# Top-k search of a sparse attention: which query tiles ScalarE searches, and where the mask is finished

## The chip, the cores and the metric

The program runs on one core of a Trainium2 chip. The metric is the device time of one execution in microseconds (us). Three runs of the kernel before were timed: the median is 2041.14 us (2039.17 to 2042.02).

## The reference

One decoder layer over 1024 tokens of width 1024: a mixer with four branches and a gated convolutional FFN, each behind an RMS norm. The branch that matters here (D) is a sparse attention. Eight small indexer heads give every query a score for every earlier key; the 256 best keys of each query are kept, ties broken towards the lower index; then four heads attend to the kept keys alone:

```python
score = jnp.einsum('bqhk,bqh->bqk', jax.nn.relu(logits), wi[:, t0:t1])
score = jnp.where(jnp.arange(kl)[None, None, :] <= qpos[None, :, None], score, -jnp.inf)
_, idx = lax.top_k(score, topk)          # topk = 256
k_sel = gather(k, idx)
...
p = jax.nn.softmax(jnp.where(valid, s, -jnp.inf), axis=-1)
```

The other inputs of the four branches are slices of one projection `z = h @ w_in`.

## The kernel before

The 1024 queries are eight tiles of 128 (t = 0 to 7), and tile t sees 128(t+1) keys. Tiles 0 and 1 keep every key, so a search is needed for tiles 2 to 7, with 384 to 1024 columns each. The scores of these six tiles lie side by side in the SBUF tile `score`; `sct(t)` is tile t's part.

The 256th best score of each query (a row) is found bit by bit, without sorting. `key` holds first the upper 16 bits of the score (15 steps), then, for the rows' tied candidates, the lower 16 bits (16 steps). One step counts the row's keys that reach a trial value and keeps or drops one bit. Two engines search different tiles side by side:

- `search_v` (L611 to L621), on VectorE, takes the tiles of `V_T`, here 7, 6, 3 and 2. Per step it has one count per tile (`count`, L604 to L609, recorded as L607 with a short read of the accumulator) and three small instructions over all of its tiles (L616, L619, L620).
- `search_a` (L623 to L638), on ScalarE, takes the tiles of `A_T`, here 5 and 4. Per step and tile it has one Sign pass that sums (L634), and two 1-column instructions (L635, L636). At its end L638 hands over its thresholds as `T`.

Between the searches, L652 to L661 on VectorE count again, mark the keys equal to the threshold found so far (L656) and put the lower 16 bits of those into `key` (L659). ScalarE's second search starts from these keys and from `kq` (L627, L628). After both, L664 to L668 join the halves to one threshold `Tx`.

The loop over ties (L670 to L680) then writes the mask. Per tile: a count of what is above the threshold (L607), the keys equal to it (L674), a running sum over them (L675, a scan), the first ones up to 256 (L677), their union with those above (L679), all on VectorE, and last, on ScalarE, L680, which turns 1 and 0 into 0 and -1e30 in `score`. The attention (L684 to L730) adds that to its logits on VectorE (L710), tile 7 first.

While VectorE searches, the other engines project. `proj` (L358) takes one 128-column block of `w_in`: the block is loaded through SyncE's queue into `wraw`, ScalarE rounds it to a high part `whi` (L187), GpSimd (POOL) takes the low part `wlo` (L188), and TensorE (PE) multiplies both with the activations in two halves of 24 matmuls (L367). ScalarE empties each half out of PSUM (L526 `pl`; L536 and L537 `chi`, `czf`; L399 to L404 `sw`, `r`), and GpSimd does the rotary arithmetic (L405 to L409). `wraw`, the pair `whi`/`wlo` and the PSUM tile `mm` have two buffers each. In between TensorE runs the conditioning projections, `adaps` (L205) and `adac` (L217), with ScalarE's copy `adae` (L214) between the two.

A scheduler decides, when the program is built, in which order each engine's instructions stand; then each engine runs its own list strictly in that order, and an instruction that waits holds all that stand behind it.

Of the kernel before, what the change touches and what calls it, by code (L numbers as in the profile page):

```python
# [16 lines left out]
AF = mybir.ActivationFunctionType  # L17
OP = mybir.AluOpType
# [8 lines left out]
NT = S // P  # L27
# [4 lines left out]
NEG = -1.0e30  # L32
# [59 lines left out]
               ("inv16", 1), ("inv32", 1), ("sgn", 1), ("nb", 6), ("dn", 6), ("nn", 6)):  # L92
    PKN = _pk(_n, _w)

V_T = [7, 6, 3, 2]
A_T = [5, 4]
NV = len(V_T)


# [13 lines left out]
def tile_hybrid_block(ctx, tc, x, pos, ada, pk, cst, w_in, w_br, w_out, w_up, w_dn, out):  # L113
# [6 lines left out]
    V, G, A, PE = nc.vector, nc.gpsimd, nc.scalar, nc.tensor  # L120
# [28 lines left out]
    epsc, halfpi, onec, negc = zcol[:, 0:1], zcol[:, 1:2], zcol[:, 2:3], zcol[:, 4:5]  # L149
# [121 lines left out]
    with ExitStack() as mix:  # L271
# [11 lines left out]
        with pool("xtp", 1) as xtp, pool("adp", 8) as adp:  # L283
# [4 lines left out]
            for t in range(NT):  # L288
                xt = adp.tile([P, D], F32, name="xt", tag="w")
                dma(xt, x[t * P:(t + 1) * P, :])  # L290
                if t == 0:
# [9 lines left out]
                                op0=OP.mult, op1=OP.add)  # L301
# [15 lines left out]
            for m in range(4):  # L317
                mod_affine(m, A1, B1, "g1", pmm, "mm", stp, "st", adp)
                for j in (2 * m, 2 * m + 1):
                    V.tensor_scalar(out=xT[:, j, :], in0=xT[:, j, :], scalar1=A1[:, j:j + 1],  # L320
                                    scalar2=B1[:, j:j + 1], op0=OP.mult, op1=OP.add)
# [6 lines left out]
            for kind in ("inv16", "inv32"):  # L328
# [4 lines left out]
                                op0=OP.mult, op1=OP.add)  # L333
                V.tensor_scalar(out=kk, in0=kk, scalar1=MAGIC, scalar2=None, op0=OP.subtract)
                for c in (_C1, _C2, _C3):
                    V.scalar_tensor_tensor(out=ang, in0=kk, scalar=-float(c), in1=ang,
                                           op0=OP.mult, op1=OP.add)
                V.tensor_scalar(out=ang, in0=ang, scalar1=3.1415925, scalar2=-3.1415925,
                                op0=OP.min, op1=OP.max)
# [151 lines left out]
        with pool("scp", 1) as scp, ExitStack() as scx:  # L491
            score = scp.tile([P, NTOT], F32, name="score")
            sct = lambda t: score[:, off[t - 2]:off[t - 1]]
            with pool("iqk", 4) as iqk, pool("itm", 3) as itm:
# [5 lines left out]
                for h in range(8):  # L500
# [3 lines left out]
                    for t in range(2, NT):  # L504
# [5 lines left out]
                        if h == 0:  # L510
                            V.tensor_scalar(out=sct(t), in0=tmp[:, :n], scalar1=wiT[:, t, h:h + 1],
                                            scalar2=zcol[:, 3:4], op0=OP.mult, op1=OP.add)
# [74 lines left out]
            with pool("rad", 1) as rad, pool("radj", 1) as radj, pool("rada", 1) as rada:  # L587
                key = rad.tile([P, NTOT], BF, name="key")
                keyt = lambda t: key[:, off[t - 2]:off[t - 1]]
# [56 lines left out]
                for t in A_T + V_T:  # L646
                    c = off[t - 2]
                    V.tensor_scalar(out=keyt(t), in0=score.bitcast(BF)[:, 2 * c + 1:2 * off[t - 1]:2],
                                    scalar1=sg_[:, kc(t):kc(t) + 1], scalar2=None, op0=OP.mult)
# [17 lines left out]
                                       op0=OP.logical_shift_left, op1=OP.bitwise_or)  # L667
                V.tensor_tensor(out=Tx, in0=Ti[:, 0, :].bitcast(F32), in1=sg_, op=OP.mult)  # L668

                for t in range(2, NT):  # L670
                    n = (t + 1) * P
                    tx = Tx[:, kc(t):kc(t) + 1]
                    g_ = count(cnt, sct(t), t, tx, OP.is_gt)
                    V.tensor_scalar(out=keyt(t), in0=sct(t), scalar1=tx, scalar2=None, op0=OP.is_equal)  # L674
                    V.tensor_tensor_scan(out=sct(t), data0=ones[:, 0:1].to_broadcast([P, n]), data1=keyt(t),  # L675
                                         initial=cnt[:, kc(t):kc(t) + 1], op0=OP.mult, op1=OP.add)
                    V.scalar_tensor_tensor(out=keyt(t), in0=sct(t), scalar=float(TOPK), in1=keyt(t),  # L677
                                           op0=OP.is_le, op1=OP.mult)
                    V.tensor_tensor(out=keyt(t), in0=keyt(t), in1=g_[:, :n], op=OP.add)  # L679
                    A.activation(sct(t), keyt(t), AF.Identity, scale=-NEG, bias=negc)  # L680

            adx.close()

# [624 lines left out]
```

## Time and profile before

| | before |
|---|---|
| median of three runs | 2041.14 us |
| profiled execution: its own time | 2039.7 us |
| its span, first to last instruction | 2037.9 us |
| PE, VectorE, ScalarE, POOL busy | 89%, 63%, 45%, 37% of the span |
| mean granted TensorE clock | 0.949 |
| chain that ended last: PE, VectorE, POOL | 47%, 22%, 13% |

The steps below are told by their start in us from the first instruction of the span: the first search runs from 182 to 252, the compaction to 267, the second search to 354, the loop over ties to 388. The sparse attention's first logits come at 456. A number that a row gives in brackets at its end is the idle time of the engine just before, and what ended it.

### The profile page before, as it was taken

The numbers are of one execution on the slowest core, as the hardware profiler recorded it, in microseconds if no ns is written. First come the engines' busy times: TensorE is split into PE (matmuls) and PEld (weight loads), VectorE is DVE, ScalarE is ACT, GpSimd is POOL, SyncE is SP. The second block draws the span as 40 slices with busy tenths as digits, with TensorE's granted clock in tenths as the row PEclk, the third lists the DMA queues.
The fourth block names the chain that finished last, engine by engine and source line by source line (L and its number), as shares of the span: only waits on it lengthen the run. The fifth ranks groups of instructions, "written<-read, shape, count | busy, mean of one in ns | idle before, by whom it ended". The sixth has DMA issues, their size and how long they took to land.

```text
span 2037.9 us, 23289 instructions
## 1 busy us (share of the span) xinstructions
PE 1819.0 (89%) x8528; PEld 1406.0 (69%) x8528; DVE 1283.4 (63%) x1896; ACT 908.7 (45%) x1648; POOL 748.8 (37%) x425
## 2 busy tenths in 40 slices
PE   6888887498999999899999899589999989799998
PEld 3655665376767776677777667368777777678886
DVE  6759999505999847684013764586676766743632
ACT  5555666246555645464123454443333333343331
POOL 0102145281111110012105611587676676555440
PEclk8988989699999999899999999799999999999999
DMA  8354422444513251513123634112122212364731
GB/s 309 95 150 162 177 100 77 134 91 120 168 54 122 79 150 58 135 47 109 62 84 134 217 127 152 52 52 81 66 82 73 73 72 73 104 229 164 238 124 62
DMA packets 78307, 237.18 MB, mean 116 GB/s; under 512 B 10673, under 2 KB 14897, under 8 KB 78065
## 3 DMA queue, kind: packets, MB, share of 16 engines
q1 hardware_dynamic: 78192, 235.69, 36.1%
q8 instruction: 67, 1.10, 0.2%
q14 instruction: 48, 0.39, 0.1%
HBM read 179.82 MB, written 55.84 MB: 116 GB/s over the span
## 4 chain that ended last, share of the span: by engine, by line
PE 47%; DVE 22%; POOL 13%; DMA 9%; issue 5%; ACT 4%; SPq 0%; DVEq 0%; POOLq 0%; ACTq 0%
PE mm L367 18%; PE dps L1186 11%; DVE junkb L607 6%; POOL wblk L942 6%; DMA wr<-in_w_up 5%; PE ups L1071 4%; PE av L488 3%; PE sc L468 2%; PE yps L995 2%; DVE hc L874 2%; PE brp L927 2%; PE tr L478 2%; POOL wsum L1051 2%; POOL wr L1051 2%; POOL wlo L188 1%
## 5 line engine op out<-in xcount | busy, mean ns | idle before, releaser
L188 POOL TENSOR_TENSOR wlo<-wraw,whi 128x1024 fp32r<-128x1024 f32 x104 | 267.5, 2576 | 856.7 <-ACT whi L187 831.9
L367 PE MATMUL mm<-hH,whi 128*128 128x512 f32 x864 | 356.0, 412 | 47.0 <-ACT whi L187 29.9
L367 PE MATMUL mm<-hL,whi 128*128 128x512 f32 x864 | 353.3, 409 | 1.2 <-DVE hL L323 1.2
L367 PE MATMUL mm<-hH,wlo 128*128 128x512 f32 x864 | 351.7, 407 | 2.9 <-POOL wlo L188 2.9
L1071 PE MATMUL ups<-th,wblk 128*128 128x512 f32 x1320 | 313.3, 394 | 16.5 <-DVE th L1099 7.9
L1071 PEld LDWEIGHTS ups<-th,wblk 128*128 128x128 f32 x1320 | 250.3, 190 | 74.1 <-DVE th L1099 11.5
L367 PEld LDWEIGHTS mm<-hH,whi 128*128 128x128 f32 x864 | 167.8, 194 | 94.1 <-ACT whi L187 30.4
L367 PEld LDWEIGHTS mm<-hH,wlo 128*128 128x128 f32 x864 | 167.3, 194 | 41.4 <-POOL wlo L188 4.2
L187 ACT CAST whi<-wraw 128x1024 fp32r<-128x1024 f32 x122 | 127.5, 1048 | 149.5 <-DMA wraw<-in_w_dn 60.8
L367 PEld LDWEIGHTS mm<-hL,whi 128*128 128x128 f32 x864 | 168.3, 195 | 36.4 <-issue 2.6
L942 POOL TENSOR_TENSOR wblk<-wr,wblk 128x512 fp32r<-128x512 f32 x84 | 137.3, 1654 | 33.1 <-ACT wblk L941 33.0
L1071 PE MATMUL ups<-h2h,wblk 128*128 128x512 f32 x352 | 124.1, 416 | 26.5 <-DVE ub L1141 25.6
L1200 DVE TENSOR_TENSOR actl<-actw,acth 128x512 fp32r<-128x512 f32 x42 | 65.2, 1578 | 105.7 <-ACT acth L1199 105.7
L607 DVE TENSOR_SCALAR_CACHE_REDUCE junkb<-key,cf 128x1024 bf16<-128x1024 uint16 (+3 forms) x124 | 117.3, 946 | 4.3
L1186 PE MATMUL dps<-wlo,acth 128*128 128x512 f32 x336 | 104.0, 389 | 0.6 <-POOL wlo L188 0.6
L1186 PE MATMUL dps<-whi,acth 128*128 128x512 f32 x336 | 104.0, 389 | 0.0
L1186 PE MATMUL dps<-whi,actl 128*128 128x512 f32 x336 | 103.9, 389 | 0.0
L1071 PEld LDWEIGHTS ups<-h2h,wblk 128*128 128x128 f32 x352 | 69.5, 198 | 49.4 <-DVE ub L1141 32.3
L941 ACT CAST wblk<-wsum 128x512 fp32r<-128x512 f32 x66 | 38.8, 618 | 143.3 <-DVE wsum L1051 142.6
L1128 DVE SCALAR_TENSOR_TENSOR ub<-ub,pkt 128x1023 f32<-128x1023 f32 x44 | 79.0, 1796 | 24.7 <-ACT ub L1127 24.7
L1127 ACT ACTIVATE ub<-ub,pkt 128x1024 f32<-128x1024 f32 x44 | 54.5, 1238 | 89.2 <-DMA act_s<-ub 76.4
L942 POOL TENSOR_TENSOR wblk<-wsum,wblk 128x512 fp32r<-128x512 f32 x66 | 91.8, 1404 | 0.0
(592 smaller groups left out, 3498.5 us busy)
## 6 DMA issues: line engine op xcount, KB each, us to landing
wraw<-in_w_in SPq DMA_DIRECT2D x54, 512.0 KB, 4.0
adaw<-in_ada SPq DMA_DIRECT2D x48, 512.0 KB, 5.8
wr<-in_w_up SPq DMA_DIRECT2D x44, 512.0 KB, 3.3
wraw<-in_w_dn SPq DMA_DIRECT2D x44, 512.0 KB, 3.5
sg_s<-gt SPq DMA_DIRECT2D x44, 256.0 KB, 2.4
sgl<-sg_s SPq DMA_DIRECT2D x22, 512.0 KB, 3.4
act_s<-ub SPq DMA_DIRECT2D x22, 512.0 KB, 2.6
actw<-act_s SPq DMA_DIRECT2D x42, 256.0 KB, 4.1
```

The lines of the kernel that those rows point to most:

```text
L187: A.copy(hi, raw)
L188: (E or G).tensor_tensor(out=lo, in0=raw, in1=hi.bitcast(F32), op=OP.subtract)
L367: PE.matmul(ps, a[:, ks], b[:, k, cs], start=(n == 0), stop=(n == 3 * NK - 1))
L488: PE.matmul(av[64 * hh:64 * hh + 64, :], vals[hh](kt), aTs[hh][:, kt, :], start=(kt == 0), stop=(kt == t), tile_position=(0, 64 * hh))
L607: V.tensor_scalar(out=j[:, :n], in0=src, scalar1=scal, scalar2=None, op0=op, op1=OP.add, accum_out=dst[:, kc(t):kc(t) + 1])
L942: E.tensor_tensor(out=b[:, 1], in0=r, in1=b[:, 0].bitcast(F32), op=OP.subtract)
L1051: tt = lambda E, o, a, b, op: E.tensor_tensor(out=o, in0=a, in1=b, op=op)
L1071: PE.matmul(ps, u[:, ks], v[:, k, :], start=(n == 0), stop=(n == 11))
L1127: A.activation(u, c, AF.Identity, bias=pc("fb", m, m + 1), scale=w(2))
L1128: V.scalar_tensor_tensor(out=u[:, 1:], in0=c[:, 0:S - 1], scalar=w(1), in1=u[:, 1:], op0=OP.mult, op1=OP.add)
L1186: PE.matmul(ps[:, cs], a[:, tl], b[:, cs], start=(chunk == 0 and n == 0 and i == 0), stop=(chunk == len(CH) - 1 and n == len(ops) - 1 and ...
L1200: V.tensor_tensor(out=lo, in0=raw, in1=hi.bitcast(F32), op=OP.subtract)
```

## The change

```diff
-V_T = [7, 6, 3, 2]
-A_T = [5, 4]
+V_T = [6, 4, 3, 2]
+A_T = [7, 5]
...
-                for t in range(2, NT):
+                for t in range(NT - 1, 1, -1):
                     n = (t + 1) * P
                     tx = Tx[:, kc(t):kc(t) + 1]
                     g_ = count(cnt, sct(t), t, tx, OP.is_gt)
...
                     V.tensor_tensor(out=keyt(t), in0=keyt(t), in1=g_[:, :n], op=OP.add)
-                    A.activation(sct(t), keyt(t), AF.Identity, scale=-NEG, bias=negc)
+                    V.tensor_scalar(out=sct(t), in0=keyt(t), scalar1=-NEG, scalar2=NEG, op0=OP.mult, op1=OP.add)
```

ScalarE searches tiles 7 and 5 (1024 and 768 columns) in place of 5 and 4 (768 and 640). VectorE searches 6, 4, 3 and 2. The loop over ties goes from tile 7 down to tile 2, and its last operation is VectorE's.

The order of the instructions on POOL and on SyncE does not change in a row. Three places move.

ScalarE at the end of the second search (`T_2702` is the second search's thresholds, `whi` the next block of weights, `chi` and `czf` a projection's halves). Before:

```order
L638 ACTIVATE T_2702<-Bn 128x2
L680 ACTIVATE score<-key,zcol 128x384
L536 ACTIVATE chi<-mm 128x512
L537 ACTIVATE czf<-mm 128x512
L680 ACTIVATE score<-key,zcol 128x512
L680 ACTIVATE score<-key,zcol 128x640
L680 ACTIVATE score<-key,zcol 128x768
L680 ACTIVATE score<-key,zcol 128x896
L187 CAST whi<-wraw 128x1024 x2
L680 ACTIVATE score<-key,zcol 128x1024
L686 ACT_TABLE_LOAD
```

And now (`junka` is a Sign pass of the search):

```order
L634 ACTIVATE junka,sgs<-key,Bn 128x1024
L636 ACTIVATE Bn<-sgn,Bn 128x1
L635 ACTIVATE sgn<-sgs,kq 128x1
L634 ACTIVATE junka,sgs<-key,Bn 128x768
L636 ACTIVATE Bn<-sgn,Bn 128x1
L635 ACTIVATE sgn<-sgs,kq 128x1
L636 ACTIVATE Bn<-sgn,Bn 128x1
L638 ACTIVATE T_2702<-Bn 128x2
L686 ACT_TABLE_LOAD
L187 CAST whi<-wraw 128x1024 x2
L536 ACTIVATE chi<-mm 128x512
L537 ACTIVATE czf<-mm 128x512
```

The six L680 are gone, and the two `whi` stand right behind the thresholds and a table load; the halves `chi` and `czf` that stood behind the first L680 now stand in the search, some rows ahead of this piece.

ScalarE between the two searches (`T_2701` is the first search's thresholds; `adae` is what TensorE's `adac` waits for). Before:

```order
L638 ACTIVATE T_2701<-Bn 128x2
L526 ACT_TABLE_LOAD
L526 ACTIVATE pl<-mm 128x512
L634 ACTIVATE junka,sgs<-key,Bn 128x768
L634 ACTIVATE junka,sgs<-key,Bn 128x640
L187 CAST whi<-wraw 128x1024
L526 ACTIVATE pl<-mm 128x512
L214 COPY adae<-adaps 128x512
L222 COPY md<-adac 128x4
L635 ACTIVATE sgn<-sgs,kq 128x1 x2
```

And now:

```order
L638 ACTIVATE T_2701<-Bn 128x2
L634 ACTIVATE junka,sgs<-key,Bn 128x1024
L526 ACTIVATE pl<-mm 128x512
L634 ACTIVATE junka,sgs<-key,Bn 128x768
L187 CAST whi<-wraw 128x1024
L526 ACTIVATE pl<-mm 128x512
L635 ACTIVATE sgn<-sgs,kq 128x1 x2
L214 COPY adae<-adaps 128x512
L636 ACTIVATE Bn<-sgn,Bn 128x1 x2
L222 COPY md<-adac 128x4
L634 ACTIVATE junka,sgs<-key,Bn 128x1024
```

The second search's first Sign pass stands ahead of a projection's `pl`, and `adae` now stands behind L635, which waits for `kq`.

VectorE's loop over ties, its first rows. Before:

```order
L668 TENSOR_TENSOR Tx<-Ti,sg__2698 128x6
L607 TENSOR_SCALAR junkb,cnt<-score,Tx 128x384
L674 TENSOR_SCALAR key<-score,Tx 128x384
L674 TENSOR_SCALAR key<-score,Tx 128x512
L675 SCALAR_TENSOR_TENSOR score<-ones,cnt,key 128x384
L674 TENSOR_SCALAR key<-score,Tx 128x640
L677 SCALAR_TENSOR_TENSOR key<-score,key 128x384
L674 TENSOR_SCALAR key<-score,Tx 128x768
L679 TENSOR_TENSOR key<-key,junkb 128x384
L674 TENSOR_SCALAR key<-score,Tx 128x896
```

And now:

```order
L668 TENSOR_TENSOR Tx<-Ti,sg__2698 128x6
L607 TENSOR_SCALAR junkb,cnt<-score,Tx 128x1024
L674 TENSOR_SCALAR key<-score,Tx 128x1024
L674 TENSOR_SCALAR key<-score,Tx 128x896
L675 SCALAR_TENSOR_TENSOR score<-ones,cnt,key 128x1024
L674 TENSOR_SCALAR key<-score,Tx 128x768
L677 SCALAR_TENSOR_TENSOR key<-score,key 128x1024
L674 TENSOR_SCALAR key<-score,Tx 128x640
L679 TENSOR_TENSOR key<-key,junkb 128x1024
L674 TENSOR_SCALAR key<-score,Tx 128x512
L680 TENSOR_SCALAR score<-key 128x1024
```

The widest tile comes first, each tile ends with its L680, and behind the loop VectorE's list is the same as before.

## Rows read from the trace of the kernel before

**Rows 1.** What TensorE waited for, 166 to 460 us: total, times, longest.

```profile
PE mm L367 <- ACT whi L187: 29.9, 1, 29.9
```

**Rows 2.** TensorE's timeline, 348 to 380 us: start, duration (us).

```profile
379.53 0.80 PE L367 MATMUL mm<-hH,whi 128*128 128x512 f32 x1 [29.93 <-ACT whi L187]
```

**Rows 3.** ScalarE's timeline behind the second search.

```profile
346.62 0.20 ACT L638 ACTIVATE T<-Bn 128x2 f32<-128x2 f32 x1
358.71 0.62 ACT L680 ACTIVATE score<-key,zcol 128x384 f32<-128x384 bf16 x1 [11.89 <-DVE key L679]
359.23 0.58 ACT L536 ACTIVATE chi<-mm 128x512 fp32r<-128x512 f32 x1
...
377.50 1.04 ACT L680 ACTIVATE score<-key,zcol 128x896 f32<-128x896 bf16 x1 [4.16 <-DVE key L679]
378.45 1.98 ACT L187 CAST whi<-wraw 128x1024 fp32r<-128x1024 f32 x2
...
388.36 1.28 ACT L686 ACT_TABLE_LOAD   x1
```

**Rows 4.** The chain that ended last, 355 to 400 us: start, duration.

```profile
360.38 1.36 POOL czf L538
...
362.88 5.34 DMA wraw<-in_w_in
```

**Rows 5.** Groups by line and shape, 150 to 460 us: busy us, mean ns, idle before.

```profile
L607 DVE TENSOR_SCALAR_CACHE_REDUCE junkb<-key,cf 128x1024 bf16<-128x1024 uint16 x16 | 20.5, 1279 | 0.5
...
L634 ACT ACTIVATE junka<-key,Bn 128x768 bf16<-128x768 uint16 x16 | 14.8, 925 | 15.8 <-DVE key L659 15.8
...
L634 ACT ACTIVATE junka<-key,Bn 128x640 bf16<-128x640 uint16 x16 | 13.1, 818 | 1.2 <-DVE key L659 1.2
...
L607 DVE TENSOR_SCALAR_CACHE_REDUCE junkb<-key,T 128x640 bf16<-128x640 int16 x1 | 0.9, 879 | 0.0
```

**Rows 6.** ScalarE's timeline between the searches.

```profile
254.80 0.93 ACT L634 ACTIVATE junka<-key,Bn 128x768 bf16<-128x768 uint16 x1 [15.80 <-DVE key L659]
...
259.31 0.57 ACT L214 COPY adae<-adaps 128x512 f32<-128x512 f32 x1
...
268.60 0.48 ACT L635 ACTIVATE sgn<-sgs,kq 128x1 f32<-128x1 f32 x2 [6.54 <-DVE kq L628]
```

**Rows 7.** What ScalarE waited for in the second search, 268 to 347 us.

```profile
ACT rhi L408 <- POOL r L407: 10.3, 4, 3.4
...
ACT rhi L437 <- POOL r L436: 4.5, 2, 2.5
```

**Rows 8.** VectorE's timeline: loop over ties, and the attention's first logits.

```profile
354.69 0.61 DVE L607 TENSOR_SCALAR_CACHE_REDUCE junkb<-score,Tx 128x384 bf16<-128x384 f32 x1
...
375.71 1.09 DVE L677 SCALAR_TENSOR_TENSOR key<-score,key 128x896 bf16<-128x896 f32 x1
376.84 0.62 DVE L679 TENSOR_TENSOR key<-key,junkb 128x896 bf16<-128x896 bf16 x1
...
381.21 3.18 DVE L677 SCALAR_TENSOR_TENSOR key<-score,key 128x1024 bf16<-128x1024 f32 x1
384.42 2.74 DVE L679 TENSOR_TENSOR key<-key,junkb 128x1024 bf16<-128x1024 bf16 x1
456.91 1.22 DVE L710 CUSTOM_DVE_ANT_0 pd<-sc,score 128x1024 f32<-128x1024 f32 x1 [69.75 <-PE sc L468]
```

**Rows 9.** POOL's timeline, 378 to 400 us.

```profile
379.55 7.06 POOL L188 TENSOR_TENSOR wlo<-wraw,whi 128x1024 fp32r<-128x1024 f32 x2 [17.83 <-ACT whi L187]
...
397.52 2.41 POOL L188 TENSOR_TENSOR wlo<-wraw,whi 128x1024 fp32r<-128x1024 f32 x1 [3.98 <-ACT whi L187]
```

**Rows 10.** Busy us (and instructions) by stretch: PE, PEld, DVE, ACT, POOL; clock, DMA.

```profile
379.50:456.00 76.50, 70.07 (x290) 56.24 (x291) 7.59 (x3) 26.87 (x40) 53.91 (x35) 0.94 0.47 111
415.00:431.00 16.00, 16.00 (x72) 13.12 (x71) 0.00 (x0) 5.77 (x9) 14.38 (x11) 1.00 0.40 102
```

**Rows 11.** A VectorE operation with two scalars, 128x1024, elsewhere in the kernel (min/median/max ns).

```profile
L1010 DVE TENSOR_SCALAR xt<-xt,sm x8: 745/752/753, 1208.8 to 1289.7; 128x1024 f32<-128x1024 f32 x8
```

## The prediction

> **What bounds the kernel now.** I read the waits of TensorE first, because TensorE leads the chain that ended last. Between the search and the attention one wait stands out: TensorE is held once for 29.9 us by ScalarE's `whi` [rows 1], up to 379.53 [rows 2]. ScalarE's timeline says why [rows 3]. Its search is over at 346.62 (L638). Then comes the first L680, which waits 11.89 us for VectorE's loop over ties, and the next ones, of which the fifth waits 4.16. The `whi` that TensorE needs stands behind them in ScalarE's list and runs at 378.45, right behind the fifth L680 (377.50). ScalarE does almost nothing in these 32 us; it is held by the order of its list.
>
> The chain of waits names a second hold in the same place [rows 4]: the weights for that `whi` were loaded late too. Their transfer (362.88, 5.34 us, so landed at 368.2) stands in SyncE's queue behind the store of a projection half, which needed POOL's `czf` (360.38), which needed ScalarE's `chi` (359.23), which stood behind the first L680 [rows 3]. From `chi` to the landing it is 9.0 us. From the landing to `whi` at 378.45 another 10 us pass in ScalarE's list.
>
> VectorE is not what the attention waits for: behind its loop it sits idle for 69.75 us until TensorE delivers the first logits at 456.91 [rows 8]. In that stretch (379.5 to 456) TensorE is busy for 70.07 of 76.5 us and POOL for 53.91 [rows 10]. So whatever moves the restart of TensorE moves the attention, and behind the attention no engine's list changes.
>
> **Part one, the split of the tiles.** VectorE counts 640 columns in place of 1024. The 1024 count takes 1279 ns and the 640 one 879 [rows 5], so a step is 0.40 us shorter: 15 x 0.40 = 6.0 us in the first search, 16 x 0.40 = 6.4 in the second. ScalarE's passes take 818 and 925 ns for 640 and 768 columns [rows 5], 107 ns for each 128, so 1024 columns take an estimated 1139. Tiles 7 and 5 in place of 5 and 4 are 384 columns more, 0.32 us a step.
>
> In the first search ScalarE's 15 x 0.32 = 4.8 us cost nothing: it was done early and then idle for 15.80 us, until VectorE's compaction let it begin again at 254.80 [rows 6]. That cover shrinks by 6.0 + 4.8 to about 5; if it were gone, ScalarE would set the start of the second search. So VectorE's 6.0 us count in full, and the second search, which waits for `kq` at 268.60 [rows 6], begins near 262.6. It may come out shorter where a small VectorE instruction must sit out a POOL pass of 2.41 us [rows 9]: I take 0 and keep 2.4.
>
> In the second search ScalarE becomes the last. VectorE would end 12.4 us earlier, at 342.3 where the loop over ties now starts at 354.69 [rows 8]. ScalarE ends 6.0 earlier by its start, and later by its 15 longer steps behind `kq`, 4.8. Some of this falls into six waits for POOL that it has anyway, 10.3 + 4.5 = 14.8 us [rows 7]; between 0 and 4.8 I take 1.5, since most steps stand outside of them. One thing is added: `adae`, which ran at 259.31 [rows 6], now stands behind L635 and so behind `kq`, near 263.1. That makes TensorE's `adac` 3.8 us later, and TensorE's next halves come back to ScalarE. Several Sign passes stand between, so I take 2 from 0 to 3.8. The thresholds then come at 346.6 - 6.0 + 4.8 - 1.5 + 2.0 = 345.9.
>
> **Part two, the mask's last operation.** In ScalarE's list `whi` now stands behind the thresholds (0.20) and the table load (1.28) [rows 3], so it runs near 347.4 instead of 378.45: 31.0 us earlier. The weights must be there too: the `chi` half ahead of their transfer now stands five Sign passes before the end, which with their small instructions and the table load are some 9 us of ScalarE, as long as the 9.0 us from `chi` to the landing. So this hold goes along with the other, give or take 2 us. Nothing on TensorE is cheaper; it only starts earlier.
>
> On VectorE the six L680 are new: 4224 columns. A two-scalar operation on 1024 fp32 columns took 752 ns [rows 11], a count 1279 [rows 5], so they cost 3.1 to 5.3 us in all; I take 4. They are hidden: the loop takes 32.5 us now (354.69 to 387.16 [rows 8]) and would run from about 346.9 to 383.4 without disturbance, while TensorE reaches the attention near 428. This is 45 us of cover. Without it each us would be paid in full.
>
> **The ties from the widest tile down** price at nothing: the attention begins with tile 7, but its L710 stands behind the whole loop on VectorE either way, and that cover is the same 45 us.
>
> **What is new in the overlap.** The loop now runs beside POOL's work for the projections. The rows show what that costs. L677 on 1024 columns took 3.18 us where 896 took 1.09, and L679 took 2.74 where 896 took 0.62 [rows 8]; meanwhile two `wlo` took 7.06 us [rows 9] where one alone takes 2.41. So both sides lose: VectorE about 2 us per meeting, POOL 7.06 - 4.82 = 2.2 over two passes, 46%. This pair of meetings is in the trace already, and the loop meets it again. What is new are meetings in the rotary part, where POOL was busy for 14.38 of 16 us [rows 10]. At 46% that could cost up to 6.6 us, and nothing if POOL has slack; the loop should leave in the middle of it, so I take 2.5.
>
> The Trainium skill, page "SBUF — State Buffer", section "SBUF: two separate sides", speaks against this change: VectorE and GpSimd share one pair of ports as an exclusive lock, and the one that comes second is blocked for the other's whole instruction. By that rule VectorE's loop and POOL's passes would be strung one behind the other, which is the first rival below. The trace agrees that an instruction can be held out for long (L677 for some 2 us [rows 8]), but not for every kind: the second search's 16 counts of 1024 columns, many of them beside POOL's passes, average 1279 ns [rows 5], so nothing is added to them.
>
> **The sum.** -31.0 + 2.5 = -28.5 us. The profiled execution took 2039.7 us (its span 2037.9), so it would take 2011.2. The median of the three runs is 1.4 us above that execution: 2012.6, said as 2013.
>
> Ends: with all of ScalarE's longer steps absorbed, `adae` free and no loss on POOL, the thresholds come at 340.6 and the gain is 36.3: 2005. With 2.4 lost in the first search, nothing absorbed, `adae` at 3.8 and POOL at 6.6, the thresholds come at 351.6, `whi` at 353.1, and the gain is 25.3 - 6.6 = 18.7: 2022.
>
> **Rivals.**
>
> *VectorE's loop becomes the end.* If the loop and POOL's 53.91 us [rows 10] never overlap, the loop ends at 346.9 + 36.5 + 53.9 = 437.3 and L710 comes there instead of 428.4. The gain falls to 19.6: 2021.5. For it speaks the 3.18 us of L677; against it, that the counts show no such wait [rows 5] and that most of POOL's 53.9 us lie behind the loop's first half, as the gaps of 3.98 and more ahead of its passes there tell [rows 9]. Chance 8%.
>
> *The weights stay late.* If SyncE's transfer lands at 368.2 as before [rows 4], `whi` gains only 10.2 us: 2031. Against it: its `chi` no longer stands behind an L680. Chance 6%.
>
> *Slower: the lock's handover.* The place is again VectorE's loop, now 36 instructions. Strung one behind the other as in the first rival, it ends at 437.3; the attention is later than before only from 456.9 on, that is when each handover costs over 0.54 us on top. At 1.0 us each the loop ends at 473.3 and the program takes 16.4 us longer: 2057. For it: meetings cost both sides, as above. Against: no row shows a handover that costs apart from the other's instruction. Chance 4%.
>
> *Nothing changes* (2041) if the gain is taken back behind the attention. Every engine's list is the same there, and I see no row for it: 2%.
>
> **How the numbers follow.** My forecast's own range, 2005 to 2022, has 77%, and 3% lies below it (both searches shorter, and TensorE's restart at the full rate). With the first rival's 8% and a little of the way to the second, the range 2004 to 2024 holds somewhat over 80%. A measurement of this kernel can tell about 0.2%, 4 us, from no change. Faster: 77 + 3 + 8 + 6 = 94%; within 0.2%: 2%; slower: 4%.
>
> **What the profile will show.** Right, if TensorE's wait of 29.9 us for `whi` is gone or below 15 us, if L638 of the second search is at 342 to 352 with `whi` 1.5 us behind, if VectorE waits for ScalarE's `T` before L665, if the six L680 on VectorE cost 3 to 5 us, and if L710 comes at 420 to 438, still behind a wait for TensorE of 20 us or more. Wrong, if `whi` waits for its transfer, if L710 directly follows the last L680, or if the stretch from L710 to the end, now 2037.9 - 456.9 = 1581.0 us, is longer by more than 3 us.

## The result and the profile after

| | before | after |
|---|---|---|
| median of four runs | 2040.16 us | 2013.91 us (2011.03 to 2016.98) |
| ratio, 95% interval | | 0.9876 (0.9850 to 0.9901) |
| profiled execution, span | 2037.9 us | 2010.4 us |
| first logits of the attention (L710) | 456.91 | 429.95 |
| from there to the end | 1581.0 us | 1580.45 us |

Forecast: 2013.0 us, 2004 to 2024. Of the 27.5 us by which the span is shorter, 456.91 - 429.95 = 26.96 lie ahead of L710.

What TensorE waited for from 160 to 440 us (total, times, longest), and the start of its work behind the second wait. To [rows 1, 2]:

```profile
PE adac L217 <- ACT adae L214: 15.3, 2, 11.4
PE mm L367 <- ACT whi L187: 14.7, 1, 14.7
```

```profile
352.51 0.80 PE L367 MATMUL mm<-hH,whi 128*128 128x512 f32 x1 [14.73 <-ACT whi L187]
```

The wait of 29.9 us for `whi` is one of 14.7. The waits for `adae` are not new. The kernel before, in the same stretch:

```profile
PE adac L217 <- ACT adae L214: 21.2, 3, 13.8
```

They have shrunk by 5.9 us, and the longest one belongs to another copy now. Both kernels have twelve copies `adae` in ScalarE's list. The longest wait before was for the eleventh, at 259.31 [rows 6]; the longest now is for the twelfth. The twelfth copy in the kernel before, then the eleventh and the twelfth in the changed kernel:

```profile
278.12 0.57 ACT L214 COPY adae<-adaps 128x512 f32<-128x512 f32 x1
```

```profile
240.42 0.59 ACT L214 COPY adae<-adaps 128x512 f32<-128x512 f32 x1 [0.44 <-PE adaps L205]
...
267.68 0.56 ACT L214 COPY adae<-adaps 128x512 f32<-128x512 f32 x1
```

So the eleventh comes 18.9 us earlier, because in ScalarE's list it now stands ahead of the first search's thresholds (a fourth place that moved), and the twelfth comes 10.4 us earlier, although it now stands behind `kq`.

ScalarE's timeline (start, duration, idle before and its cause), between the searches and behind the second. To [rows 6, 3]:

```profile
267.30 0.48 ACT L635 ACTIVATE sgn<-sgs,kq 128x1 f32<-128x1 f32 x2 [8.30 <-DVE kq L628]
...
349.89 0.20 ACT L638 ACTIVATE T<-Bn 128x2 f32<-128x2 f32 x1
350.12 1.28 ACT L686 ACT_TABLE_LOAD   x1
351.41 1.04 ACT L187 CAST whi<-wraw 128x1024 fp32r<-128x1024 f32 x1
353.55 1.04 ACT L187 CAST whi<-wraw 128x1024 fp32r<-128x1024 f32 x1 [1.09 <-DMA wraw<-in_w_in]
```

The thresholds come at 349.89, 3.3 us later than before, but the table load and `whi` follow at once: `whi` runs at 351.41 where it ran at 378.45, 27.04 us earlier. The second `whi` waits 1.09 us for its transfer, so the weights land only just in time; TensorE has no second wait for `whi`.

VectorE's loop over ties, and the first logits. To [rows 8]:

```profile
350.13 0.17 DVE L665 CAST Ti<-T 128x6 int32<-128x6 f32 x1 [2.09 <-ACT T L638]
...
350.74 1.28 DVE L607 TENSOR_SCALAR_CACHE_REDUCE junkb<-score,Tx 128x1024 bf16<-128x1024 f32 x1
...
355.31 4.45 DVE L675 TENSOR_TENSOR_SCAN score<-ones,cnt,key 128x1024 f32<-128x1024 f32 x1
...
362.78 0.68 DVE L680 TENSOR_SCALAR score<-key 128x1024 f32<-128x1024 bf16 x1
...
368.67 2.71 DVE L680 TENSOR_SCALAR score<-key 128x896 f32<-128x896 bf16 x1
...
397.27 1.34 DVE L680 TENSOR_SCALAR score<-key 128x384 f32<-128x384 bf16 x1
429.95 1.22 DVE L710 CUSTOM_DVE_ANT_0 pd<-sc,score 128x1024 f32<-128x1024 f32 x1 [31.34 <-PE sc L468]
```

VectorE now waits for ScalarE's thresholds (2.09). The loop runs from 350.74 to 398.61 (the last L680 is over then), 47.9 us. It is hidden: the attention comes 31.34 us later, still behind TensorE's `sc`.

POOL's timeline beside the loop. To [rows 9]:

```profile
352.53 5.08 POOL L188 TENSOR_TENSOR wlo<-wraw,whi 128x1024 fp32r<-128x1024 f32 x2 [8.66 <-ACT whi L187]
...
368.43 2.47 POOL L188 TENSOR_TENSOR wlo<-wraw,whi 128x1024 fp32r<-128x1024 f32 x1 [3.81 <-ACT whi L187]
...
386.49 2.21 POOL L405 TENSOR_TENSOR r<-r,cosinv 128x512 f32<-128x512 f32 x1
```

The two `wlo` take 5.08 us where they took 7.06. Later passes, such as this L405, are longer than their usual 1.3 us. From `whi` to L710 it is 78.54 us; before, 78.46.

### The profile page after: what moved, and what is told of

Read it like the earlier page. It is cut to its first block, busy times and chain, and to the rows that moved or that the text cites. A ratio compares the mean times of both kernels' runs of the same rounds, so it can differ in the third digit from the quotient of the medians.

```text
span 2010.4 us, 23289 instructions
## 1 busy us (share of the span) xinstructions
PE 1815.1 (90%) x8528; PEld 1402.7 (70%) x8528; DVE 1292.4 (64%) x1902; ACT 913.8 (45%) x1642; POOL 749.8 (37%) x425
## 3 DMA queue, kind: packets, MB, share of 16 engines
q1 hardware_dynamic: 78192, 235.69, 36.6%
## 4 chain that ended last, share of the span: by engine, by line
PE 49%; DVE 18%; POOL 14%; DMA 8%; ACT 6%; issue 4%; SPq 0%; DVEq 0%; POOLq 0%; ACTq 0%
PE mm L367 18%; PE dps L1186 11%; POOL wblk L942 6%; DMA wr<-in_w_up 5%; PE ups L1071 5%; DVE junkb L607 3%; PE sc L468 3%; PE av L488 3%; PE yps L995 2%; DVE hc L874 2%; PE brp L927 2%; PE tr L478 2%; POOL wsum L1051 2%; POOL wr L1051 2%; POOL wlo L188 1%
## 5 line engine op out<-in xcount | busy, mean ns | idle before, releaser
L367 PE MATMUL mm<-hH,whi 128*128 128x512 f32 x864 | 355.1, 411 | 33.9 <-ACT whi L187 14.7
L607 DVE TENSOR_SCALAR_CACHE_REDUCE junkb<-key,cf 128x896 bf16<-128x896 uint16 (+3 forms) x124 | 104.9, 846 | 4.2
```

The costliest lines, as they stand in the source:

```text
L367: PE.matmul(ps, a[:, ks], b[:, k, cs], start=(n == 0), stop=(n == 3 * NK - 1))
L607: V.tensor_scalar(out=j[:, :n], in0=src, scalar1=scal, scalar2=None, op0=op, op1=OP.add, accum_out=dst[:, kc(t):kc(t) + 1])
```

## The experiments

The change has three parts, and each was run alone on the kernel before, and two of them together. Then one suspected cost, VectorE's waits for POOL, was changed by itself, and after that the order of the work that still holds `whi`.

| kernel | us, median | ratio to before, 95% |
|---|---|---|
| mask's last operation alone | 2022.89 | 0.9921 (0.9902 to 0.9940) |
| division of the search alone | 2022.72 | 0.9924 (0.9901 to 0.9946) |
| order of the ties alone | 2033.79 | 0.9971 (0.9959 to 0.9984) |
| mask and division | 2013.97 | 0.9878 (0.9859 to 0.9898) |
| the changed kernel once more | 2010.68 | 0.9864 (0.9849 to 0.9878) |
| change, `wlo` in four pieces | 2002.85 | 0.9825 (0.9807 to 0.9844) |
| change, `kq` ahead | 2008.23 | 0.9852 (0.9828 to 0.9875) |
| change, `kq` ahead and pieces | 1996.16 | 0.9802 (0.9779 to 0.9826) |
| change, all weight loads ahead | 2057.00 | 1.0087 (1.0071 to 1.0104) |
| change, four loads ahead | 2019.93 | 0.9909 (0.9881 to 0.9936) |
| pieces, `kq`, four loads | 2007.06 | 0.9845 (0.9831 to 0.9860) |
| the same, first query loads ahead | 2013.71 | 0.9869 (0.9852 to 0.9885) |

### The mask alone

```diff
-                    A.activation(sct(t), keyt(t), AF.Identity, scale=-NEG, bias=negc)
+                    V.tensor_scalar(out=sct(t), in0=keyt(t), scalar1=-NEG, scalar2=NEG, op0=OP.mult, op1=OP.add)
```

> Of the change only the mask's last operation on VectorE; the split (7,6,3,2 and 5,4) and the ties' order as before. My theory, ScalarE's list: the time is set by when the two weight casts (L187) behind the second search start. Here the second search still ends near 346.6 us, and the casts stand behind the table load and behind the evictions of the key projection's second half (chi, czf), whose store stands in front of the weights' load in SyncE's list. In the kernel before the weights were on the chip 9.0 us after that chi; chi at 348 to 350, so the casts at 357 to 359, PE restarting at 358 to 360 instead of 379.5: 20 us less, about 2020 us (2016 to 2025). Rival, the mask alone is the whole gain: 2012. Rival, the search's new division is the gain: 2040, no change.

Measured 2022.89. ScalarE's timeline behind the second search:

```profile
347.56 0.20 ACT L638 ACTIVATE T<-Bn 128x2 f32<-128x2 f32 x1
...
349.07 0.60 ACT L536 ACTIVATE chi<-mm 128x512 fp32r<-128x512 f32 x1
...
357.60 1.04 ACT L187 CAST whi<-wraw 128x1024 fp32r<-128x1024 f32 x1 [7.43 <-DMA wraw<-in_w_in]
```

From `chi` to `whi` it is 8.53 us, and ScalarE waits 7.43 of them for the transfer. This is the second hold of the forecast, seen alone: with the L680 gone, `chi` still stands behind the thresholds, and the weights behind `chi`'s store. L710 comes at 438.8, 18.1 us earlier than before. My theory gave 20 and the two rivals 28 and 0.

### The division alone

```diff
-V_T = [7, 6, 3, 2]
-A_T = [5, 4]
+V_T = [6, 4, 3, 2]
+A_T = [7, 5]
```

> Of the change only the division of the search (ScalarE tiles 7 and 5); mask on ScalarE, ties from the narrowest up. ScalarE's list: the first weight cast now stands right behind the thresholds, near 350, the second behind the mask of the narrowest tile (near 358), and the projection's evictions and the third weight cast behind masks of wider tiles (512 and 640, then 768 and 896), each of which waits for VectorE's tie loop. PE restarts near 351, but is held again: the third cast comes about 375 instead of 367 in the changed kernel (396 before). So about 20 us less than before, 2020 (2014 to 2028). Rival, the division alone is the gain (VectorE's tie loop starts earlier or ScalarE's share fits better): 2013. Rival, the division loses 4.8 us of ScalarE's time and gains nothing: 2045.

Measured 2022.72. ScalarE's timeline:

```profile
351.53 1.03 ACT L187 CAST whi<-wraw 128x1024 fp32r<-128x1024 f32 x1
358.27 0.62 ACT L680 ACTIVATE score<-key,zcol 128x384 f32<-128x384 bf16 x1 [5.71 <-DVE key L679]
358.79 1.03 ACT L187 CAST whi<-wraw 128x1024 fp32r<-128x1024 f32 x1
...
379.10 1.04 ACT L680 ACTIVATE score<-key,zcol 128x896 f32<-128x896 bf16 x1 [4.16 <-DVE key L679]
...
381.00 1.04 ACT L187 CAST whi<-wraw 128x1024 fp32r<-128x1024 f32 x1
```

The first `whi` is as early as in the changed kernel, but the third stands behind the mask of 896 columns and runs at 381.00 (367.30 in the changed kernel). The evictions `chi` and `czf` stand behind masks too, and they are what TensorE waits for there (1.6 us, once, in the changed kernel):

```profile
PE mm L367 <- ACT czf L537: 9.9, 4, 3.3
```

The gain is a place in a list again. It is not the division of the work: this kernel gives ScalarE more to search, and its thresholds are later than before (351.42 against 346.62).

The two parts alone gain 18 us each, together 27. They don't add because they work on the same stall: with the mask alone `whi` still waits for its weights, with the division alone the first `whi` is free but the evictions and the third `whi` still stand behind masks.

### The ties alone

```diff
-                for t in range(2, NT):
+                for t in range(NT - 1, 1, -1):
```

> Of the change only the ties from the widest tile down; mask on ScalarE, old division. ScalarE's list: both weight casts stand behind the masks of the tiles of 1024, 896, 768 and 640, four of six and the longest, so they start at 380 to 385 (378.5 before): between no change and 7 us longer, 2040 to 2047. Rival, the order matters because the first consumer (tile 7) gets its mask first: some us less than before, 2030 to 2038.

Measured 2033.79, a miss: I expected no gain. ScalarE's timeline has `whi` behind four L680, as foreseen, and no earlier than before:

```profile
378.03 0.83 ACT L680 ACTIVATE score<-key,zcol 128x640 f32<-128x640 bf16 x1 [2.96 <-DVE key L679]
378.76 1.98 ACT L187 CAST whi<-wraw 128x1024 fp32r<-128x1024 f32 x2
```

L710 comes at 457.1 (456.91 before), and the profiled execution took 2038.3 us, 1.4 less than that of the kernel before. It is not one of the seven executions out of ten that took 2032 to 2034 us, so its trace can't show the 7 us of the medians; where they are saved stays open. The next run shows no part of them in the change's gain.

### Mask and division without the ties

> The change without the ties' order. ScalarE's list is instruction for instruction that of the changed kernel, and VectorE's tie loop ends some 30 us before its first consumer, whichever tile comes last: the same time as the changed kernel, 2013 (2010 to 2017), PE restarting near 352.5. Rival, the order of the ties bears a part of the gain: 2018 or more.

Its diff is the two pieces above together. Measured 2013.97, the changed kernel's time, and TensorE's wait is the same:

```profile
PE mm L367 <- ACT whi L187: 14.7, 1, 14.7
```

So the order of the ties adds nothing that these times show to the other two parts.

### VectorE's waits for POOL: `wlo` in four pieces

The forecast's largest miss was the first search: 6.0 us shorter by its counts, it began the second only 1.3 us earlier (`sgn` at 267.30 against 268.60). The groups of the first search (busy us, mean ns, idle before) say where the rest is. Kernel before:

```profile
L619 DVE TENSOR_TENSOR ge<-cnt,kreq 128x4 f32<-128x4 f32 x15 | 2.4, 163 | 0.5
```

Changed kernel, with the count of 896 columns beside it:

```profile
L607 DVE TENSOR_SCALAR_CACHE_REDUCE junkb<-key,cf 128x896 bf16<-128x896 int16 x15 | 17.2, 1146 | 0.5
...
L619 DVE TENSOR_TENSOR ge<-cnt,kreq 128x4 f32<-128x4 f32 x15 | 7.5, 502 | 0.5
```

The 4-column L619 lost 7.5 - 2.4 = 5.1 us in 15 steps. This is no accident of one execution: in the seven kept traces with the new division and `wlo` in one piece, L619 took 5.4 to 9.8 us in the first search, in the three with the old division 2.4 to 2.8. In the changed kernel's timelines one of them, on VectorE and on POOL:

```profile
240.14 2.30 DVE L619 TENSOR_TENSOR ge<-cnt,kreq 128x4 f32<-128x4 f32 x1
242.48 0.16 DVE L620 SCALAR_TENSOR_TENSOR T<-ge,T 128x4 f32<-128x4 f32 x1
```

```profile
240.06 2.36 POOL L188 TENSOR_TENSOR wlo<-wraw,whi 128x1024 fp32r<-128x1024 f32 x1 [10.34 <-ACT whi L187]
```

L619 begins 0.08 us behind `wlo` and ends 0.02 behind it (242.44, 242.42). The test cuts `wlo`:

```diff
-        (E or G).tensor_tensor(out=lo, in0=raw, in1=hi.bitcast(F32), op=OP.subtract)
+        for c in range(0, D, 256):
+            (E or G).tensor_tensor(out=lo[:, c:c + 256], in0=raw[:, c:c + 256], in1=hi[:, c:c + 256].bitcast(F32),
+                                   op=OP.subtract)
```

> The changed kernel with GpSimd's subtraction for the weights' low part (wlo, L188) issued as four pieces of 256 columns instead of one of 1024. In the trace of the changed kernel VectorE's small L619 at 240.14 lasts 2.30 us and ends at 242.44, where GpSimd's wlo (240.06, 2.36 us) ends; three others (199.76, 213.40, 226.80) end with a wlo too. My theory: such an instruction sits out the rest of the GpSimd instruction that is running. Then no L619 that meets a wlo lasts over 0.8 us, its mean falls from 586 ns to 250 to 400 ns, the first search on VectorE ends some 4 us earlier, and with it kq, adae and the second thresholds: 2010 (2006 to 2014). Rival: the wait is to the end of GpSimd's whole run of work, whatever its pieces: the same waits of 1.0 to 2.3 us, time 2013 to 2017 (the pieces cost GpSimd some 0.3 us each weight).

Measured 2002.85, under the range of either theory. The changed kernel ran beside it once more:

> The changed kernel once more, beside the three above: 2014 (2010 to 2018).

Measured 2010.68, so the pieces gain 7.8 us. The same place, on VectorE and on POOL (four pieces in one row), and the group of the first search:

```profile
238.41 0.44 DVE L621 TENSOR_TENSOR ge<-cnt,kreq 128x4 f32<-128x4 f32 x1
238.89 0.66 DVE L622 SCALAR_TENSOR_TENSOR T<-ge,T 128x4 f32<-128x4 f32 x1
239.58 0.66 DVE L618 TENSOR_SCALAR cf<-T 128x4 f32<-128x4 f32 x1
```

```profile
238.11 2.79 POOL L189 TENSOR_TENSOR wlo<-wraw,whi 128x256 fp32r<-128x256 f32 x4 [10.34 <-ACT whi L187]
```

```profile
L621 DVE TENSOR_TENSOR ge<-cnt,kreq 128x4 f32<-128x4 f32 x15 | 3.1, 207 | 0.5
```

Each small instruction here sits out at most one piece, and the next may meet the next piece: 0.44, 0.66 and 0.66 in place of 2.30. So a part of what L619 gets back is paid by the two behind it: over the first search the three together take 10.3 us, where they took 12.6 in the changed kernel and 7.6 before. L619's mean in the first search falls from 502 to 207 ns, over both searches from 586 to 311 (its longest, 1.27 us, is in the second search beside the rotary passes, which were not cut). The second search's first Sign pass begins 6.8 us earlier (247.20 against 253.97): 2.9 are there when the first search begins (its `kq` starts at 178.59, not 181.47), 1.6 come from `kq` itself (0.72 us, not 2.35) and 2.3 from the three small instructions. `whi` comes 5.1 us earlier and L710 4.05. The rival, waits for POOL's whole run of work, is out: POOL ran the four pieces back to back.

The span is 12.1 us shorter, so in these two executions 8 more come behind L710, where `wlo` is computed for later weights as well. The medians differ by 7.8 to 11.1 us: the execution profiled is the fastest of its four. Its granted clock was also the highest, 0.961 against 0.956 in the changed kernel's, but the clock is not the whole of it: at 0.956 the kernel in pieces took 2000.89 and 2004.81 us, the changed kernel 2009.90 to 2012.20. One place of it is the convolution (L874, here L876). First the changed kernel, then the one in pieces (min/median/max ns, first to last start):

```profile
L874 DVE SCALAR_TENSOR_TENSOR hc<-hpad,pkt,hc x60: 1250/1270/3448, 497.5 to 652.5; 128x1024 f32<-128x1024 f32 x60
```

```profile
L876 DVE SCALAR_TENSOR_TENSOR hc<-hpad,pkt,hc x60: 1248/1269/1805, 491.9 to 643.0; 128x1024 f32<-128x1024 f32 x60
```

Its longest instruction falls from 3448 to 1805 ns, and its last one comes 9.5 us earlier where its first came 5.6. The remaining 2.6 us (12.1 - 9.5) were not followed.

### `kq` ahead

```diff
-                for t in A_T + V_T:
+                for t in A_T:
                     count(cnt, keyt(t).bitcast(I16), t, T1[:, kc(t):kc(t) + 1], OP.is_gt)
...
-                V.tensor_tensor(out=kreq, in0=kreq, in1=cnt, op=OP.subtract)
+                V.tensor_tensor(out=kreq[:, NV:NB], in0=kreq[:, NV:NB], in1=cnt[:, NV:NB], op=OP.subtract)
                 search_a(T2, U16, 16)
+                for t in V_T:
...
+                V.tensor_tensor(out=kreq[:, 0:NV], in0=kreq[:, 0:NV], in1=cnt[:, 0:NV], op=OP.subtract)
                 search_v(T2, U16, 16)
```

> The changed kernel with ScalarE's part of the second search's start (remaining count and kq for tiles 7 and 5) computed as soon as these two tiles are prepared, instead of behind all six. Theory: in the changed kernel ScalarE's first small step of the second search waited 8.3 us for kq, and adae (and PE, 11.4 us) behind it. Now it starts near 257 instead of 267.3, PE's wait for adae falls to under 4 us, PE's projections and ScalarE's thresholds come 8 us earlier (T near 342), and so do the evictions in front of the weights' load, whi near 343 to 346: 2006 (2003 to 2010). Rival: the weights' arrival, behind the store of the low part, bounds whi at 350 whatever ScalarE does: 2012 to 2015. Rival: VectorE's end, 348, bounds it: 2012.

Measured 2008.23, against 2010.68 for the changed kernel beside it (2013.91 at first): 2.5 to 5.7 us, less than the 8 foreseen. ScalarE's timeline:

```profile
257.39 0.48 ACT L635 ACTIVATE sgn<-sgs,kq 128x1 f32<-128x1 f32 x2 [0.17 <-DVE kq L628]
...
342.10 0.20 ACT L638 ACTIVATE T<-Bn 128x2 f32<-128x2 f32 x1
...
346.46 1.04 ACT L187 CAST whi<-wraw 128x1024 fp32r<-128x1024 f32 x1 [2.85 <-DMA wraw<-in_w_in]
```

The 8.3 us of idle time are gone and the thresholds come at 342.10, as foreseen. But `whi` waits 2.85 us for its weights, so it gains 5.0 of 7.8. TensorE's longest wait for `adae` is 7.5 us, not under 4. Theory and first rival each hold for a part.

### Both

> The changed kernel with both: kq ahead (ScalarE starts the second search 8 us earlier) and wlo in four pieces. In the run with kq alone whi waited for the weights (2.85 us behind the table load). Theory: thresholds near 337, 5 us earlier again, but the weights' arrival holds whi at 342 to 346, so the two gains don't add in full: 2000 (1997 to 2003), against 2002.9 and 2008.2 alone. Rival: they add, 1997 or less.

Measured 1996.16, 0.9802 (0.9779 to 0.9826): the fastest here, ahead of the kernel before by 2.0% and of the changed one by 14 to 18 us. From the thresholds to `whi`:

```profile
335.60 0.20 ACT L640 ACTIVATE T<-Bn 128x2 f32<-128x2 f32 x1
...
339.93 1.04 ACT L187 CAST whi<-wraw 128x1024 fp32r<-128x1024 f32 x1 [2.83 <-DMA wraw<-in_w_in]
```

The weights hold `whi` again, by 2.83 us, and still the rival (they add, 1997 or less) fits better: 14.5 us under 2010.68, alone 7.8 and 2.5 to 5.7. With executions from 1993.7 to 2003.5 us, that they add in full is not clear of the noise. ScalarE's evictions came earlier along with everything else (thresholds at 335.60, not 337), and so did the weights.

### Loads ahead: four kernels that gave the gain back

The weights stand in SyncE's list behind the store of a projection half. The first try gave every projection's load priority when the lists are made:

```diff
-        dma(raw, src)
+        with tc.high_priority(2000):
+            dma(raw, src)
```

> The changed kernel with the weight loads of the projections given priority where the lists are made: in SyncE's list the weights for the second half of the query and key projections stand in front of the first half's stores instead of behind, and their casts stand within the second search. Theory: PE's wait of 14.7 us for whi goes, ScalarE's thresholds come later by the evictions that now fall into the search (some 20 us, T near 370), VectorE's tie loop has that much of its 31 us of slack left to lose, and the widest tile, first in the loop, is ready near 380: first attention reduction near 415 instead of 430, 1999 (1992 to 2010). Rival: SyncE is held by loads that wait for a weight buffer, the stores and adaw loads behind them come late, PE waits there instead: 2013 to 2030. Rival: the late thresholds bound the attention: 2013 or more.

Measured 2057.00. The loads pulled the projections ahead of the indexer's scores too, and the first search began 36.6 us later. VectorE's first `kq` (L627, here L628), at 181.47 in the changed kernel, and its first L710 (here L711):

```profile
218.04 2.32 DVE L628 TENSOR_TENSOR kq<-pkt,kreq 128x2 f32<-128x2 f32 x1
...
454.04 1.22 DVE L711 CUSTOM_DVE_ANT_0 pd<-sc,score 128x1024 f32<-128x1024 f32 x1
```

The second search began 67.5 us later (its first Sign pass at 321.45, not 253.97). The first logits come without idle time behind VectorE's loop over ties, 24.1 us later than in the changed kernel: the second rival.

So only the four loads around the stall were moved:

```diff
-        raw = wr.tile([P, D], F32, name="wraw", tag="w")
-        dma(raw, src)
+        with tc.high_priority(pri):
+            raw = wr.tile([P, D], F32, name="wraw", tag="w")
+            dma(raw, src)
...
-            hi, lo = split_w(w_in[W_INDEX[(name, i)]])
+            hi, lo = split_w(w_in[W_INDEX[(name, i)]],
+                             pri=300 if (name, i) in (("qc", 1), ("kc", 1), ("qb", 0), ("kb", 0)) else 0)
```

> The changed kernel with priority for four weight loads alone (second query and key projection of the one branch, first of the next), so that SyncE issues them as soon as a weight buffer is free, ahead of the stores they stood behind; the casts of the first two weights stand in ScalarE's list among the second search's steps, all other loads as in the changed kernel. Theory: the 14.7 us in which PE waits for whi was the rest of a bound by the weights' place in two lists; PE's wait for whi falls under 3 us, T comes 4 to 6 us later by the evictions that move ahead of it (353 to 356), first attention reduction near 417 to 420 instead of 430: 2000 (1996 to 2006). Rival: SyncE is held by loads that wait for a buffer and the attention's loads come late, PE's sc waits for a DMA: 2008 or more. Rival: later thresholds make VectorE's tie loop the bound: 2010 or more.

Measured 2019.93: the first rival. TensorE's wait and VectorE's first two L710 (here L712):

```profile
PE sc L470 <- DMA qds<-qk_s: 19.2, 1, 19.2
```

```profile
418.32 1.22 DVE L712 CUSTOM_DVE_ANT_0 pd<-sc,score 128x1024 f32<-128x1024 f32 x1 [8.69 <-DMA qk_s<-sw]
...
446.59 1.22 DVE L712 CUSTOM_DVE_ANT_0 pd<-sc,score 128x1024 f32<-128x1024 f32 x1 [10.63 <-PE sc L470]
```

The wait for `whi` is gone and the first logits come at 418.32, as foreseen. Then TensorE waits 19.2 us for `qds`: in SyncE's new list two of the attention's query loads stand behind all the rotary stores.

> kq ahead, wlo in pieces and the four loads ahead together. Theory: with the weights' arrival out of the way the gains add: 2000 less 10 to 13, 1988 (1983 to 1996), PE's waits for whi under 3 us in all. Rival: another wait takes its place (PE for the evictions on ScalarE, or SyncE for buffers): 1997 or more.

Measured 2007.06: the rival; the same wait, 19.1 us. Last, these query loads were moved ahead as well:

```diff
+                            with tc.high_priority(3000 if pr == 0 else 0):
```

> The last kernel (kq ahead, wlo in pieces, four weight loads ahead) with priority also for the loads of the attention's first queries (qds), which in the two kernels with the weight loads ahead had fallen in SyncE's list behind the rotary stores: PE's sc waited 19.2 us for them, and that undid the gain. Theory: with both waits gone (19.2 for qds, 11.5 for whi) the time falls under that of the kernel with kq and pieces alone (1996): 1985 (1978 to 1993). Rival: the softmax of the widest tile now stands in ScalarE's list ahead of weight casts and evictions and waits there for VectorE's mask, PE waits for those instead: 1996 or more.

Measured 2013.71: the rival. ScalarE's timeline, and TensorE's waits:

```profile
383.38 1.15 ACT L734 ACTIVATE pd<-pd,sm 128x1024 f32<-128x1024 f32 x1 [23.89 <-DVE sm L733]
```

```profile
PE mm L371 <- ACT czf L541: 26.7, 3, 17.4
```

The softmax of tile 7 now stands ahead of evictions and weight casts in ScalarE's list, and holds them for 23.89 us until VectorE's mask and L710 are done. TensorE waits 17.4 us for `czf`.

## Why the prediction was right, point by point

- **What bounds.** Right. `whi` came 27.04 us earlier, L710 26.96, and behind L710 nothing changed (1580.45 against 1581.0). The runs of the parts show the two holds that the forecast named, ScalarE's list and the weights behind `chi`'s store, each alone.
- **First search, 6.0 us shorter.** Mis-sized: 1.3. The step that failed is the term for small VectorE instructions that must sit out a POOL pass, "I take 0 and keep 2.4". They lost 5.1 us, because four of five `wlo` now fall on L619 (the fifth on `kq`, as in the kernel before); before, in the same stretch, none did (mean 163 ns). The run in pieces shows this cause, though it wins back only 2.3 of the 5.1 us here.
- **Second search, 5.3 us longer on ScalarE.** 4.6 (267.30 to 349.89, 82.6; before 78.0). The estimate of 1139 ns for 1024 columns was right (1137 to 1140 measured). ScalarE was the last, as foreseen.
- **`adae`, 3.8 us later, for 2.0 on the thresholds.** Wrong in sign. The copy that ran at 259.31 is not the one that now stands behind `kq`: that is the twelfth, which ran at 278.12, and it came 10.4 us earlier. TensorE's waits for `adae` fell from 21.2 to 15.3 us. No run shows the 2.0 us; that the second search's sum came out near all the same is luck as far as this term goes.
- **`whi` 1.5 us behind the thresholds.** Right: 1.52. The weights were there in time for the first `whi`; the second waited 1.09 us, so the margin was small.
- **Six L680 for 4 us, 3.1 to 5.3.** 6.2, above the range: undisturbed the widest takes 0.68, but the one of 896 took 2.71 beside a `wlo`. They are hidden, as forecast, as is the whole loop (47.9 us, not 36.5).
- **POOL, 2.5 us.** Mis-sized: 0.1. The two `wlo` met the loop in a better order (5.08, not 7.06) and later passes in a worse one. That the two cancel is a reading of POOL's rows; no run separates them.
- **The sum.** -27.04 + 0.1 against -31.0 + 2.5. Two terms missed in opposite directions, by 4.0 and 2.4 us, so that the time is nearer than the terms is luck.
- **The signs.** Two did not come as forecast: the six L680 cost 6.2 us, not 3 to 5, and a `whi` (the second) waited for its transfer. TensorE's wait, the thresholds, VectorE's wait for `T`, L710 and the rest behind it came as said.
- **Rivals.** VectorE's loop was over 31 us before its first consumer, so neither the first rival nor the slower one came. The Trainium skill, page "SBUF — State Buffer", section "Who interferes with whom", tells apart which VectorE operations take the pair of ports that GpSimd uses: those with two SBUF inputs do, and the form of `tensor_scalar` that also writes out its accumulator does not. The forecast had told the rule without this condition, and found the exception of the counts in its own rows. The trace agrees with the condition: L619 (two inputs) sat out `wlo`, while the counts (the other form) average 1146 ns on 896 columns in a search with five `wlo`.

## What to carry to other kernels

Where an engine idles for a long time, read its own list before its producers: the wait here was a place in ScalarE's list, and behind it one in SyncE's, and two edits that work on the same stall don't add. After each edit, read on all lists what has moved ahead of what; three kernels here removed the wait they aimed at and lost it again to a load or a softmax that had changed its place. Some small VectorE instructions in a serial loop beside GpSimd (here L619 and, beside the pieces, the two behind it; not the counts) can pay the rest of the GpSimd instruction that is running, so cutting that instruction into pieces can pay even though GpSimd's own work gets longer.

## What the runs showed that I had not expected

- A shorter loop can lose what it saved to its phase: 0.40 us less a step made four of five `wlo` fall on L619, which then took up to 2.30 us in place of 0.16.
- Four pieces cost POOL 2.79 us in place of 2.36, and the program gained 8 us by the medians. In the two traces compared, two thirds of the gain lie behind the stretch for which the pieces were meant.
- A row that looks like the same instruction in two timelines can be another one: `adae` at 267.68 looks 8.4 us late against the one at 259.31, but counted from the first copy on its counterpart is the one at 278.12, and it is 10.4 us early.
